# Forty-two split matmuls in the last block, and six sums moved within one early period

## The chip, the cores and the metric

The kernel runs on one core of one Trainium2 chip. The metric is the device time of one execution in microseconds, the median of several executions. A profile was taken of one execution of each kernel. Its times are counted from the first instruction, and its span leaves out about 2 us of the execution that lie outside the program's own instructions.

## The reference

A dense layer, an exact GELU, and a second dense layer:

```python
def reference(x, w1, b1, w2):           # x 16 x 512 x 768, w1 768 x 3072, w2 3072 x 768, fp32
    y = np.matmul(x, w1) + b1
    y = 0.5 * y * (1.0 + erf(y / np.sqrt(2.0)))
    return np.matmul(y, w2).astype(np.float32)
```

## The kernel before

The kernel works in fp16 and saves matmuls by a Strassen scheme: seven products in place of eight, with sums of blocks made on VectorE (DVE). The rows go in eight blocks of 1024 (`sb`). In a block (the first two differ in part) stage 1 has twelve units (`k`) of seven products, each three matmuls of 512 columns. The last stage has seven units of seven products, each twelve matmuls of 192 columns. TensorE (PE) runs the products in periods that mix the unit `i` that begins with the unit `j` that ends:

```python
def period(i, j, fill):            # (cut: special cases)
    p1(i); copy_xy(i)              # bank bX, then bX copied into bY
    p7(j); fill(1)                 # bank bY of j, then add_c22 reads it
    p5(i); fill(2)                 # bW
    p3(j); fill(3)                 # bZ, then a sum reads it
    p6(i); j.right_done(); fill(4) # bank bY of i; then it is copied into bZ
    p4(j); fill(5)                 # bY of j
    p2(i); fill(6)                 # bX
```

`fill(slot)` puts work for DVE and the queues between the products. DVE takes its work in the order of the program, as the DVE lines of e1 below show, where a copy stands behind sums that waited 1.19 us for a load. These sums belong to one early period, the one before W1 tile 6 is first used (`at[1, 0]` is 7, so the period is `pos == 5`):

```python
if slot == (1 if pos < at[1, 0] else 4) and pos + 1 < len(seq) and seq[pos + 1][0] == 0:
    prep_wt(seq[pos + 1][1])                       # 4 sums of the next W1 tile
...
if slot == 1:
    if pos == at[1, 0] - 2:
        x_sums(1, soon, slice(0, RH // 2), (0, 1)) # 2 sums of x of block 1
```

The last unit of the last block (`ends`) writes its results out in pieces as they are done:

```python
def p3(u):                                         # (cut)
    u.mm(3, bZ, False, 0, u.C)
    nc.vector.tensor_tensor(out=u.c12(), ...)
    if u.ends:
        u.store(0)                                 # 384 KB, nc.sync
...
def last(self, banks):                             # (cut) the last two stores, 96 KB each
    (nc.sync, nc.scalar)[t].dma_start(out=orr[...], in_=o)
```

Of the kernel before, what the change touches and what calls it, by code (L numbers as in the profile page):

```python
# [22 lines left out]
def kernel(  # L23
# [8 lines left out]
    nc = tc.nc  # L32
# [5 lines left out]
    RH = SB // 2  # L38
    nsb = R // SB
# [81 lines left out]
    def w1_op(wt, slot):  # L121
        raw = wt[:, 0:4 * KQ * P].rearrange("p (a k b c) -> p a b k c", a=2, k=KQ, b=2)
        if slot in RAW:
            return raw[:, RAW[slot][0], RAW[slot][1]]
        return wt[:, slot * KQ * P:(slot + 1) * KQ * P].rearrange("p (k c) -> p k c", c=P)
# [79 lines left out]
    with tc.manual_schedule():  # L205

        soon, queue, late, slow = [], [], [], []

        def tt(o, a, b, op):
            nc.vector.tensor_tensor(out=o, in0=a, in1=b, op=op)  # L210

        def later(n, f, q=None):
            (queue if q is None else q).append((70 + n * 0.52, f))

        def sums(ns):

            for q in (soon, queue):
                while q and ns >= q[0][0] * 0.6:
                    ns -= q[0][0]
                    q.pop(0)[1]()  # L220

        def flush(q):
            while q:
                q.pop(0)[1]()
# [18 lines left out]
        def keep(n):  # L243
            nc.sync.dma_start(out=w1s[hi_of(n)][:], in_=wts[n])

        def prep_wt(n, ks=()):
            o = {s: w1_op(wts[n], s) for s in range(7)}
            early = ((T3, B22, T1, SUB), (T2, T3, B11, ADD), (T4, B21, T2, SUB), (T1, T1, B11, SUB))
            usual = ((T3, B22, T1, SUB), (T1, T1, B11, SUB), (T2, B22, T1, SUB), (T4, B21, T2, SUB))
            for d, a, b, op in [early[k] for k in ks] if ks else usual:  # L250
                later(KQ * P, lambda d=d, a=a, b=b, op=op: tt(o[d], o[a], o[b], op), soon)
# [6 lines left out]
        def prep_w2(d, c, q):  # L258
            a, b = {T1: (T3, B11), T2: (B22, T1), T3: (B22, T3), T4: (B21, T2)}[d]
            o = [w2v[s][:, :, c:c + W2C, :] for s in (d, a, b)]  # L260
            later(2 * W2C * N4, lambda: tt(*o, SUB), q)
# [69 lines left out]
        def transpose_pe(sb, t, copy=nc.scalar.copy):  # L331
            for kc in range(2 * KQ):
                nc.tensor.transpose(out=bT[t % 2][:, kc, :], in_=xhs[t][:, kc * P:(kc + 1) * P],
                                    identity=ident[:])
            copy(out=xT_of(sb, t), in_=bT[t % 2][:])  # L335

        def blocks(sb):
            XT = XTs[sb]
            return [XT[:, a, c:c + KQ, :] for a in range(2) for c in (0, KQ)]

        def x_sums(sb, q, r=slice(0, RH), ks=range(4)):
            A11, A12, A21, A22 = [a[:, :, r] for a in blocks(sb)]
            S1, S2, S4 = [a[:, :, r] for a in XSs[sb]]
            n = KQ * len(range(RH)[r])
            ops = ((S1, A21, A22, ADD), (S2, S1, A11, SUB), (A21, A11, A21, SUB), (S4, A12, S2, SUB))
            for k in ks:
                later(n, lambda k=k: tt(*ops[k]), q)

        def g_sum(k, U, c0=0, c1=NH, q=None):
            G1, G2 = g_of(U // NU)  # L350
            r = slice(U % NU * P, (U % NU + 1) * P)
            g11, g21 = G1[:, c0:c1, 0, r], G1[:, c0:c1, 1, r]
            g12, g22 = G2[:, c0:c1, 0, r], G2[:, c0:c1, 1, r]
            s = [t[:, c0:c1, :] for t in GS]
            a, b, op = ((g21, g22, ADD), (s[0], g11, SUB), (g11, g21, SUB), (g12, s[1], SUB))[k]
            later((c1 - c0) * P, lambda: tt(s[k], a, b, op), q)
# [40 lines left out]
        class Unit1:  # L397
# [11 lines left out]
            def mm(self, p, dst, first, c0, c1):  # L409
                A11, A12, A21, A22 = blocks(self.sb)  # L410
                a, slot = {1: (A11, B11), 2: (A12, B21), 3: (self.XS[2], B22), 4: (A22, T4),
                           5: (self.XS[0], T1), 6: (self.XS[1], T2), 7: (A21, T3)}[p]
                for c in range(c0, c1):
                    nc.tensor.matmul(out=dst[:, 0:RH], lhsT=w1_op(self.wt, slot)[:, c, :],  # L414
                                     rhs=a[:, c, :], start=first and c == 0,
                                     stop=c == self.C - 1, skip_group_check=True)

            def alloc(self):
                self.tmp = (tmps1 if self.sb < ONE else
# [325 lines left out]
        for half in range(2):  # L745
            r = slice(half * KQ, (half + 1) * KQ)
# [36 lines left out]
        def plain(n, row, side, half, r=slice(0, RH)):  # L783
            slot = ((B11, T1), (B21, B22))[half][side]
            for c in range(KQ):
                nc.tensor.matmul(out=banks[n, row][side][:, r], lhsT=w1_op(wts[n], slot)[:, c, :],
                                 rhs=blocks(0)[2 * row + half][:, c, r],
                                 start=half == 0 and c == 0 and r.start == 0,
                                 stop=half == 1 and c == KQ - 1, skip_group_check=True)

        def plain_done(n, row, side):
            nc.scalar.activation(out=Gs[0][side][:, n, row, :], in_=banks[n, row][side][:, 0:RH],
                                 func=GELU, bias=b1t[:, 2 * n + side:2 * n + side + 1])
# [41 lines left out]
        for k in (2, 3):  # L835
            for r in (top, bottom):
# [5 lines left out]
        seq = ([(0, k) for k in range(7)] +  # L842
               [(1, 0), (1, 1), (1, 2), (0, 7), (1, 3), (0, 8), (1, 4), (0, 9), (1, 6), (0, 10), (0, 11),
                (1, 5), (1, 10), (1, 11), (1, 7), (1, 8), (1, 9)])
        at = {u: n for n, u in enumerate(seq)}
# [10 lines left out]
        def loads_a(pos):  # L856
            if pos == 0:
                load_wt(4)
                load_next_x(1, (0, 4, 1, 5))
                load_wt(5)  # L860
                load_next_x(1, (2, 6, 3, 7))
                load_wt(6)
            for n in range(7, NH):
                if pos == at[1, over[n]] + 1:
                    load_wt(n)
            if pos in w2_at_pos:
                load_w2(*w2_at_pos[pos])
# [6 lines left out]
        def transposes_a(pos):  # L874
            for t in (pos - 1, pos + 3):
                if t not in X1_PE:
                    transpose_dma(1, t)

        def fill_a(pos, slot):
            if pos == 2 and slot == 1:  # L880
                plain(1, 1, 1, 1, bottom)
                plain_done(1, 1, 1)
            if (pos, slot) in X1_AT:
                transpose_pe(1, X1_PE[X1_AT.index((pos, slot))])
            if pos == at[1, 0] - 1 and slot == 2:
                x_sums(1, soon, slice(RH // 2, RH), (0, 1))
            if slot == (1 if pos < at[1, 0] else 4) and pos + 1 < len(seq) and seq[pos + 1][0] == 0:
                prep_wt(seq[pos + 1][1])
            if slot == 4:
                if pos in (3, 4):  # L890
                    prep_wt(pos - 3, (3,))
                for m, c in ((21, 9), (22, 0), (23, 3), (23, 6)):
                    if pos == m:
                        prep_w2(T2, c, queue)
                        prep_w2(T3, c, late if m == 23 else queue)
                if pos == 23:
                    for c in range(0, NH, W2C):
                        prep_w2(T4, c, late)
            if slot == 1:
                if pos == at[1, 0] - 2:  # L900
                    x_sums(1, soon, slice(0, RH // 2), (0, 1))
                if pos == at[1, 0]:
                    x_sums(1, soon, ks=(2, 3))
                if pos == at[0, NH - 1] + 2:
                    for c in range(0, NH, W2C):
                        prep_w2(T1, c, queue)
                    for k in (0, 1):
                        g_sum(k, 0)
            if pos > at[0, NH - 1]:
                if slot in (1, 4):  # L910
                    sums((0, 1100, 0, 0, 1500)[slot])
            elif slot in (1, 2, 4, 5):
                sums((0, 600, 300, 0, 600, 300)[slot])
            if slot == 5:
                loads_a(pos)
                if pos < 5:
                    transposes_a(pos)
                for n in KEEP.get(pos, ()):
                    keep(n)
            if slot == 6:  # L920
                flush(soon)
# [256 lines left out]
```

## Time and profile before

| | kernel before |
|---|---|
| time, median of 6 runs (3 of them known at the prediction) | 852.37 us (852.18 to 852.68) |
| span of the profiled execution | 850.53 us |
| TensorE busy | 842.8 us, 99% |
| start of the last matmul | 845.02 us |
| last part of the last store landed | 849.44 us |
| last instruction fetch of TensorE | 844.30 us, 16,384 bytes, 1.24 us |

In the trace the landing of each of the last eight stores is told by 16 updates of its semaphore (a counter that other work waits for). I read them as 16 parts, one for each DMA engine; the prediction names the page that says so. The time between the fifteenth and the sixteenth update is then the time for which one engine alone holds up the whole transfer; I call it the gap.

### The profile page before, as it was taken

What the parts mean: (1) busy time and instruction counts of PE and PEld (TensorE: products, weight loads), DVE (VectorE), ACT (ScalarE), POOL (GpSimd) and SP (SyncE); (2) the same over time, 40 slices, a digit from 0 to 9 for tenths busy, and PEclk for the clock granted to TensorE, in tenths of its full rate; (3) what the DMA queues carried; (4) which work ended last, traced back from release to release, by engine and by line L of the source; (5) the groups of instructions that cost most, each with busy time, mean ns of one, the idle gap of its engine ahead of it and who ended that gap; (6) DMA issues with size and microseconds to landing.
All of it is one profiled execution on the core that took longest, in us unless ns stands there. A gap on an engine that the chain in (4) does not pass through costs nothing.

```text
span 850.5 us, 16682 instructions
## 1 busy us (share of the span) xinstructions
PE 842.8 (99%) x6504; PEld 573.4 (67%) x6504; DVE 673.3 (79%) x1134; ACT 426.3 (50%) x700; POOL 94.8 (11%) x151
## 2 busy tenths in 40 slices
PE   8999999999999999999999999999999999999997
PEld 5444445796544897449964599545995469944797
DVE  5766679777857997679967799668996699957997
ACT  4777763231287413773247721577126861277511
POOL 5021100042200002000020000210002100010000
PEclk9999999999999999999999999999999999999999
DMA  9998796699998699977999599995999949984497
GB/s 224 203 282 173 163 222 230 235 203 219 368 340 185 216 338 364 290 163 266 335 366 292 125 298 342 360 288 108 316 350 347 259 143 323 359 308 146 122 316 255
DMA packets 144819, 222.11 MB, mean 261 GB/s; under 512 B 61964, under 2 KB 85444, under 8 KB 144740
## 3 DMA queue, kind: packets, MB, share of 16 engines
q1 hardware_dynamic: 117392, 178.85, 66.6%
q0 software_dynamic: 27168, 42.08, 22.3%
q8 instruction: 51, 0.84, 0.4%
q14 instruction: 28, 0.23, 0.1%
q10 hardware_dynamic: 180, 0.11, 0.0%
HBM read 181.78 MB, written 49.45 MB: 272 GB/s over the span
## 4 chain that ended last, share of the span: by engine, by line
PE 98%; DMA 1%; ACT 0%; DVE 0%; SPq 0%; issue 0%
PE bY L414 21%; PE bY L518 15%; PE bX L414 14%; PE bX L518 10%; PE bW L414 7%; PE bZ L414 7%; PE bZ L518 5%; PE bW L518 5%; PE bY L457 4%; PE bZ L457 2%; PE bW L457 2%; PE bY L606 2%; PE bX L606 1%; PE bX L457 1%; DMA arena<-in_x_dram 1%; PE bZ L606 1%
## 5 line engine op out<-in xcount | busy, mean ns | idle before, releaser
L210 DVE TENSOR_TENSOR arena<-arena 128x1536 f16<-128x1536 f16 (+6 forms) x638 | 410.1, 674 | 5.7 <-ACT arena L335 0.9
L414 PEld LDWEIGHTS <-arena 128*128 128x128 f16 x1974 | 192.5, 98 | 224.0 <-issue 0.2
L518 PEld LDWEIGHTS <-arena 128*128 128x128 f16 x3528 | 292.1, 98 | 8.2
L414 PE MATMUL bY<-arena 128*128 128x512 f16 x846 | 214.4, 379 | 0.0
L637 DVE TENSOR_TENSOR arena<-bY,arena 128x512 f32<-128x512 f32 (+1 forms) x102 | 69.4, 681 | 118.1 <-PE bY L414 88.0
L630 ACT COPY bY<-bX 128x512 f32<-128x512 f32 (+1 forms) x145 | 79.6, 549 | 118.1 <-DVE arena L567 87.9
L518 PE MATMUL bY<-arena 128*128 128x192 f16 x1500 | 138.3, 246 | 0.0
L414 PE MATMUL bX<-arena 128*128 128x512 f16 x564 | 138.2, 379 | 0.0
L430 ACT ACTIVATE arena<-arena,b1t 128x1024 f16<-128x1024 f32 x94 | 108.0, 1149 | 51.6 <-DVE arena L665 51.6
L650 ACT COPY arena<-bW 128x512 f32<-128x512 f32 (+1 forms) x149 | 81.9, 550 | 92.9 <-PE bW L518 43.9
L518 PE MATMUL bX<-arena 128*128 128x192 f16 x1020 | 93.1, 246 | 0.0
L665 DVE TENSOR_TENSOR arena<-bZ,arena 128x512 f32<-128x512 f32 (+1 forms) x102 | 69.3, 679 | 21.4 <-PE bZ L414 18.2
L550 POOL DMA_DIRECT2D out_dram<-arena x42 | 30.5, 728 | 409.7 <-DVE arena L661 374.1
L414 PE MATMUL bW<-arena 128*128 128x512 f16 x282 | 76.2, 379 | 0.0
L414 PE MATMUL bZ<-arena 128*128 128x512 f16 x282 | 76.2, 379 | 0.0
L681 ACT COPY bZ<-bY 128x512 f32<-128x512 f32 (+1 forms) x60 | 31.8, 529 | 80.8 <-PE bY L457 30.0
L435 ACT ACTIVATE arena<-bX,b1t 128x512 f16<-128x512 f32 x94 | 64.0, 680 | 9.8 <-PE bX L414 9.7
L435 ACT ACTIVATE arena<-bY,b1t 128x512 f16<-128x512 f32 x94 | 63.3, 674 | 0.0
L457 PEld LDWEIGHTS <-arena 128*128 128x128 f16 x432 | 42.2, 98 | 28.0 <-issue 0.2
L319 POOL DMA_DIRECT2D arena<-in_x_dram x60 | 33.5, 626 | 156.3 <-DMA arena<-arena 146.9
L518 PE MATMUL bZ<-arena 128*128 128x192 f16 x504 | 48.5, 246 | 0.0
L518 PE MATMUL bW<-arena 128*128 128x192 f16 x504 | 48.5, 246 | 0.0
(63 smaller groups left out, 426.4 us busy)
## 6 DMA issues: line engine op xcount, KB each, us to landing
arena<-w2s SPq DMA_DIRECT2D x299, 288.0 KB, 4.6
arena<-w1s SPq DMA_DIRECT2D x72, 672.0 KB, 6.8
out_dram<-arena POOLq DMA_DIRECT2D x46, 384.0 KB, 7.1
w2s<-arena SPq DMA_DIRECT2D x49, 288.0 KB, 4.4
arena<-in_x_dram POOLq DMA_DIRECT2D x60, 192.0 KB, 7.7
w1s<-arena SPq DMA_DIRECT2D x12, 672.0 KB, 6.6
arena<-in_w_dram POOLq DMA_DIRECT2D x17, 384.0 KB, 8.4
out_dram<-arena SPq DMA_DIRECT2D x13, 384.0 KB, 2.5
```

Source lines behind the costliest of these rows:

```text
L210: nc.vector.tensor_tensor(out=o, in0=a, in1=b, op=op)
L319: nc.gpsimd.dma_start(out=xhs[t], in_=xr[:, sb * 8 + t, :])
L414: nc.tensor.matmul(out=dst[:, 0:RH], lhsT=w1_op(self.wt, slot)[:, c, :], rhs=a[:, c, :], start=first and c == 0, stop=c == self.C - 1, ski ...
L430: nc.scalar.activation(out=self.G[1][:, hi, :, :], in_=self.tmp, func=GELU, bias=b1t[:, 2 * hi + 1:2 * hi + 2])
L435: nc.scalar.activation(out=self.G[0][:, hi, row, :], in_=bank[:, 0:RH], func=GELU, bias=b1t[:, 2 * hi:2 * hi + 1])
L457: nc.tensor.matmul(out=dst[:, 0:N2], lhsT=a, rhs=w[:, :, c, :], start=first and c == 0, stop=c == self.C - 1, skip_group_check=True)
L518: nc.tensor.matmul(out=dst[:, t * N4:(t + 1) * N4], lhsT=a, rhs=w[:, c, :], start=first and c == 0 and t == ts[0], stop=c == NQ - 1, skip_ ...
L606: nc.tensor.matmul(out=dst[:, t * N4:(t + 1) * N4], lhsT=a, rhs=self.w[q][:, c, :], start=first and c == 0 and t == 0, stop=c == NQ - 1, s ...
L630: nc.scalar.copy(out=bY[u.g % 2][:, 0:u.F], in_=bX[u.g % 2][:, 0:u.F])
L637: nc.vector.tensor_tensor(out=u.c22(), in0=bY[u.g % 2][:, 0:u.F], in1=w[:, 0:u.F], op=ADD)
L650: nc.scalar.copy(out=w[:, 0:u.F], in_=bW[:, 0:u.F])
L665: nc.vector.tensor_tensor(out=u.c12(), in0=bZ[:, 0:u.F], in1=w[:, 0:u.F], op=ADD)
```

## The change

Its intent, in its own words, is "to shift instruction fetches". Two units of the last block run each matmul of 512 columns as two of 256, which adds 84 instructions to TensorE's stream. Besides, the sums of W1 tile 6 and of x(1) come later in their period.

```diff
+                w = RH // (2 if self.sb + 1 == nsb and self.k in (1, 2) else 1)
                 for c in range(c0, c1):
-                    nc.tensor.matmul(out=dst[:, 0:RH], lhsT=w1_op(self.wt, slot)[:, c, :],
-                                     rhs=a[:, c, :], start=first and c == 0,
-                                     stop=c == self.C - 1, skip_group_check=True)
+                    for r in range(0, RH, w):
+                        nc.tensor.matmul(out=dst[:, r:r + w], lhsT=w1_op(self.wt, slot)[:, c, :],
+                                         rhs=a[:, c, r:r + w], start=first and c == 0 and r == 0,
+                                         stop=c == self.C - 1, skip_group_check=True)
...
-            if slot == (1 if pos < at[1, 0] else 4) and pos + 1 < len(seq) and seq[pos + 1][0] == 0:
+            if slot == (1 if pos < at[1, 0] and pos != at[1, 0] - 2 else 4) and pos + 1 < len(seq) and seq[pos + 1][0] == 0:
                 prep_wt(seq[pos + 1][1])
...
+            if pos == at[1, 0] - 2 and slot == 4:
+                x_sums(1, soon, slice(0, RH // 2), (0, 1))
             if slot == 1:
-                if pos == at[1, 0] - 2:
-                    x_sums(1, soon, slice(0, RH // 2), (0, 1))
```

## The prediction

> **What bounds the kernel now.** I read the page's busy table first, then its chain of work that ended last, then the waits of TensorE, then the stretches of the last 12 us. Busy share and chain agree:
>
> ```profile
> span 850.5 us, 16682 instructions
> PE 842.8 (99%) x6504; PEld 573.4 (67%) x6504; DVE 673.3 (79%) x1134; ACT 426.3 (50%) x700; POOL 94.8 (11%) x151
> PE 98%; DMA 1%; ACT 0%; DVE 0%; SPq 0%; issue 0%
> ```
>
> A busy TensorE is not proof of a full one, because matmuls overlap. So I looked at its waits (waiter, what it waited for, us in total, times, longest) and at the spacing of its instructions in the timeline:
>
> ```profile
> PE bX L764 <- DVE arena L750: 1.2, 1, 1.2
> PE bT L333 <- DVE arena L770: 0.7, 1, 0.7
> PE bT L333 <- ACT arena L335: 0.4, 1, 0.4
> ```
>
> These three are all of its waits, and all lie in the first 10 us. From the first product to the last, six matmuls of 512 columns start 1.29 us apart (215.7 ns each) and 24 of 192 columns 1.98 us (82.5 ns each). Summed over the whole trace, the starts after 10 us are less than 1 us late against those two rates. So nothing in the middle can be gained by moving waits about. What is left is the head, which the change doesn't touch, and the tail after the last matmul (845.02 us): some 5.5 us of a last sum, the last stores and the ending.
>
> The tail, as busy time in chosen stretches (columns: stretch, length, busy of PE, weight loads, DVE, ACT, POOL, granted clock, DMA share, GB/s):
>
> ```profile
> 838.60:840.50 1.90, 1.90 (x26) 1.90 (x25) 1.90 (x4) 0.25 (x1) 0.00 (x0) 1.00 0.00 0
> 840.70:841.70 1.00, 1.00 (x15) 1.00 (x13) 0.90 (x3) 0.00 (x0) 0.00 (x0) 1.00 0.95 347
> 842.00:844.20 2.20, 2.20 (x30) 2.20 (x27) 1.85 (x5) 0.00 (x0) 0.00 (x0) 1.00 1.03 365
> ...
> 845.90:846.40 0.50, 0.00 (x0) 0.00 (x0) 0.00 (x0) 0.00 (x0) 0.00 (x0) 1.00 0.05 15
> 846.60:848.10 1.50, 0.00 (x0) 0.00 (x0) 0.00 (x0) 0.00 (x0) 0.00 (x0) 0.87 1.02 350
> 848.30:848.90 0.60, 0.00 (x0) 0.00 (x0) 0.00 (x0) 0.00 (x0) 0.00 (x0) 0.50 0.07 23
> ```
>
> A share of 0.05 to 0.07 is one DMA engine of 16. So at 845.9 and again at 848.3 fifteen engines are done and a single one works on, and the kernel ends with that one. The landings say the same. Of the store issued at 842.54, 15 parts land by 845.60 and the sixteenth at 847.39 (1.79 us later); of the next (843.91) the gap is 1.68; of the last three it is 0.73, 0.76 and 0.79, the very last part landing at 849.44 instead of 848.65. The cause I read in the DMA packets: in 842 to 852 us there is one packet of the instruction queue, 16,384 bytes, at 844.30, taking 1.24 us. The page counts them:
>
> ```profile
> q8 instruction: 51, 0.84, 0.4%
> ```
>
> The trace doesn't name the engine of a packet, so that the late engine is the one with the fetch is inferred. But the earlier fetches show the same thing: after those at 812.03 and 833.41 the last part of the next transfers lands 1.49 and 1.02 us after the fifteenth, against some 0.1 us in transfers far from a fetch.
>
> **What the Trainium skill says.** (1) "Runtime: NRT & Kernel Launch", Instruction fetch mechanics: instructions stream in through a DMA queue of the sequencer's own, in blocks of 16 KiB, which are 256 instructions, and a crossing is mostly hidden. The trace agrees on the size: 51 packets of 16,384 bytes, some 256 TensorE instructions apart, for 13,022 built ones (50.9 blocks). It is hidden from TensorE, but the tail shows it not hidden from a store. (2) "DMA: Bandwidth & Descriptors", Queues, rings and completion order: each DMA engine takes its queue rows in turn, whole packets at a time. That fits one engine held up by one fetch. (3) Same page, Why a DMA increments its semaphore by 16 and not by 1: only the full count means landed, so one late engine makes the whole store late; the 1.79 us gap is that. (4) "TensorE: Matmul & The Clock Gate", Wait — 56ns, not 53.3ns?: a matmul's spacing is its columns at 2.4 GHz plus about 2.5 ns. The trace agrees: 215.7 ns for 512, 82.5 for 192.
>
> **The change, part by part.** *Split matmuls.* Two units (k = 1, 2) of the last block have 7 products of 3 matmuls, 42 in all. Each becomes two of 256 columns: 42 matmuls and, in the built program, 42 weight loads more, 84 instructions. The cost: the 48 matmuls of 256 columns that the kernel already has (the start's) are spaced 109.2 ns, with weight loads of 98 ns in between that keep up. Two of them take 218.4 against 215.7, so 2.6 ns for each split matmul, times 42: **+0.11 us**, all of it on the path.
>
> *What the 84 instructions move.* Fetches come at fixed counts in the stream: the last four stood at 12,220, 12,474, 12,736 and 13,001 TensorE instructions started, so the last one should again come near 13,001. That was 20 instructions before the end; now it is 104. 84 instructions are 42 matmuls of 192 columns, 42 x 82.5 ns = 3.46 us earlier against the tail: at 840.8 on the old clock. There is no 52nd fetch: one block more would come near 13,257, and the stream ends at 13,106.
>
> At 840.8 the fetch meets the first of the last stores (DMA share 0.95) and delays one engine by what the others cost: 1.0 to 1.8 us. Before the last stores that engine can catch up wherever the other 15 idle. The old tail shows how much: from the store of 843.91 to that of 844.90 the gap shrank from 1.68 to 0.73, so 0.95 us, at the lull between 845.83 and 846.46. The new place adds the lull at 841.75 to 841.95, 0.2 us. Together 1.15 us. What remains at the end is 0 (fetch costs 1.0) to 0.65 us (it costs 1.8); I take 0.25, as the nearest fetches (1.02 and 1.49) are nearer the low end. In place of 0.79 us that makes **-0.54 us**, an estimate from the landings.
>
> *Sums moved within one early period.* In the built order, DVE's four sums of W1 tile 6 and the two of x(1) stand behind the two PSUM operations of their period instead of in front of and between them; no other engine's order changes (but for the longer PE stream). Before:
>
> ```profile
> 36.38 1.14 DVE L210 TENSOR_TENSOR arena<-arena 128x384 f16<-128x384 f16 x3 [0.66 <-DMA arena<-in_w_dram]
> 37.44 0.68 DVE L665 TENSOR_TENSOR arena<-bZ,arena 128x512 f32<-128x512 f32 x1
> 38.23 0.70 DVE L683 COPY bZ<-bY 128x512 f32<-128x512 f32 x1
> 38.84 1.41 DVE L210 TENSOR_TENSOR arena<-arena 128x384 f16<-128x384 f16 x3
> ```
>
> DVE waits 0.66 us for the tile's load there, with the copy into bZ queued behind. But that copy ends at 38.93 and TensorE writes bZ again at 40.61, so 1.7 us of slack, and no wait of TensorE is on the list. After: the sum from bZ runs near 36.6, the copy near 37.3, then four sums of 0.38 us and two of 0.56, ending near 40.6. T1 of tile 6 is ready near 38.8 and first used by TensorE at 39.97; the sum on bY that follows (old start 40.16) starts some 0.4 us later and ends near 41.3, and TensorE touches that bank again at 41.9. All fits. The worth in these runs: **0.0 us**. What it buys is tolerance of a late load, which the three runs (852.32 to 852.53) don't show to be needed.
>
> Sum: 852.42 + 0.11 - 0.54 + 0.0 = 851.99, say 852.0 us.
>
> **The rivals.** *A: the fetch only changes its victim.* Between 841.95 and 845.83 all 16 engines are busy without a break, so a delay taken at 840.8 can't shrink there; if it costs 1.8 us, as the one at 844.30 did, 0.65 us remains and the change gains 0.14 - 0.11, nothing: 852.4. For it: the DMA share of 1.03. Against it: 0.2 us more to catch up in, and a fetch that mostly costs nearer 1 us.
>
> *B: the late engine leaves altogether.* With a fetch that costs 1.1 us or less the whole 0.79 goes: 852.42 + 0.11 - 0.79 = 851.74. This is the floor, as the last store's other 15 parts land at 848.65 whatever the fetch does.
>
> *C: TensorE loses more than 0.11 us.* The split units double the weight loads in their 9 us, and DVE's later sums come within 0.7 us of the bank that TensorE wants. Weight loads of 98 ns against 109 of matmul speak against the first; that it would be one wait of some tenths, against a large second. It would give 852.6 to 853.0.
>
> *D: the fetches of the last block, all moved, delay a weight load.* Those loads are issued some ten products ahead (10 x 0.99 us) and land in 4.6 us, so 1.5 us of delay is hidden.
>
> **Range and chances.** B's floor with the run-to-run 0.1 us sets 851.55 at the low end; A with part of C sets 852.65 at the high end. Nearly all of what I can imagine lies within 1 us, and 2% would be 17 us, so the chances are 0.01 faster, 0.98 within 2%, 0.01 slower.
>
> **What would show it.** In the new profile: 6546 matmuls; TensorE's last matmul about 0.11 us later; one instruction packet near 840.9 and none after; the last store's sixteenth part within 0.4 us of the fifteenth, and a DMA share near 0 in the stretch after most parts landed; DVE's wait for the W1 load gone, and TensorE's waits still only those of the first 10 us. The prediction is wrong if the last fetch falls elsewhere than 3.5 us earlier, if a late engine remains although the fetch has moved (then the fetch wasn't its cause), or if TensorE shows a new wait near 40 us or in the last block.

## The result, and the profile after

| | before | after |
|---|---|---|
| time, median | 852.37 us (6 runs, 852.18 to 852.68) | 851.36 us (6 runs, 850.89 to 851.60) |
| span of the profiled execution | 850.53 | 848.74 |
| start of the last matmul | 845.02 | 844.64 |
| last store landed | 849.44 | 847.59 |
| from the last matmul's start to the last landing | 4.42 | 2.95 |
| last fetch, against the start of the last matmul | 0.73 earlier | 5.44 earlier |
| gap of the last three stores | 0.73, 0.76, 0.79 | 0.02, 0.04, 0.03 |

The ratio is 0.9987, with a 95% interval of 0.9974 to 1.0: the same within 2%. (Ratios are the mean time of one kernel's fast runs over that of the other's of the same rounds, so not quite the ratio of the medians.) The gain is 1.01 us by the medians. I had said 0.4 us, in a range from 851.55 to 852.65 us; what failed in the working is said further below.

The busy table of the page has hardly moved:

```profile
span 848.7 us, 16767 instructions
...
PE 843.3 (99%) x6546; PEld 577.6 (68%) x6546; DVE 673.5 (79%) x1134; ACT 426.4 (50%) x700; POOL 94.9 (11%) x151
```

The stretches of the tail have. These answer to the six that the prediction shows (stretch, length, busy time of PE, weight loads, DVE, ACT and POOL, granted clock, DMA share, GB/s):

```profile
838.20:840.10 1.90, 1.90 (x26) 1.90 (x24) 1.90 (x4) 0.27 (x1) 0.00 (x0) 1.00 0.04 9
840.30:841.30 1.00, 1.00 (x15) 1.00 (x13) 0.90 (x3) 0.00 (x0) 0.00 (x0) 1.00 0.95 344
841.60:843.80 2.20, 2.20 (x29) 2.20 (x28) 1.84 (x5) 0.00 (x0) 0.00 (x0) 1.00 1.01 363
...
845.50:846.00 0.50, 0.00 (x0) 0.00 (x0) 0.00 (x0) 0.00 (x0) 0.00 (x0) 1.00 1.02 359
846.00:847.10 1.10, 0.00 (x0) 0.00 (x0) 0.00 (x0) 0.00 (x0) 0.00 (x0) 1.00 0.98 340
847.30:847.90 0.60, 0.00 (x0) 0.00 (x0) 0.00 (x0) 0.00 (x0) 0.00 (x0) 1.00 0.00 0
```

Three things are to be seen. In the quiet stretch before the last stores one engine is now at work, where before there was none; the view of DMA queues for that stretch says what it does:

```profile
DMA packets 1, 0.02 MB, mean 9 GB/s; under 512 B 0, under 2 KB 0, under 8 KB 0
...
q8 instruction: 1, 0.02, 3.8%
```

It is the last fetch, alone (839.20, taking 1.15 us). Secondly, the end with one engine at work is gone: 0.00 in place of 0.07. Thirdly, so is the lull of the 15 other engines (0.05 before, at 845.90 to 846.40); at the same point of the tail the share is now 1.02. The timeline of SyncE's issues tells why the lull went. The first lines are the kernel before's (start, us, what):

```profile
844.90 1.04 SPq L550 DMA_DIRECT2D out_dram<-arena  x1
846.04 0.42 SPq L529 DMA_DIRECT2D out_dram<-arena  x1
```

And the changed kernel's:

```profile
844.52 0.37 SPq L552 DMA_DIRECT2D out_dram<-arena  x1
844.98 0.44 SPq L531 DMA_DIRECT2D out_dram<-arena  x1
```

The same store of 384 KB took 1.04 us to issue before and takes 0.37 now, and the one behind it is issued some 0.7 us sooner after the last matmul.

The spans differ by 1.79 us, more than the medians do. By matching the same matmul in both traces: 0.54 us of the difference arose before the sixty-first matmul, up to where the two programs are the same. In all 14 profiles the sixty-first matmul starts anywhere from 12.89 to 13.97 us, as the first loads land sooner or later; the profiled execution of the changed kernel was an early one and its fastest (850.89). At 43 to 45 us it lost 0.11 us in two late starts, the first 0.05 us after the end of the next copy out of bank bY, and in the two split units 0.09 us. The last matmul then came 0.39 us sooner, and the tail behind it was 1.47 us shorter.

### The profile page after: what moved, and what is told of

It reads as the page before. It is cut to its first block, busy times and chain, and to the rows that moved or that the text cites. A ratio compares the mean times of both kernels' runs of the same rounds, so it can differ in the third digit from the quotient of the medians.

```text
span 848.7 us, 16767 instructions
## 1 busy us (share of the span) xinstructions
PE 843.3 (99%) x6546; PEld 577.6 (68%) x6546; DVE 673.5 (79%) x1134; ACT 426.4 (50%) x700; POOL 94.9 (11%) x151
## 4 chain that ended last, share of the span: by engine, by line
PE 99%; DMA 1%; SPq 0%; DVE 0%; ACT 0%; issue 0%
PE bY L416 22%; PE bY L520 15%; PE bX L416 14%; PE bX L520 10%; PE bZ L416 7%; PE bW L416 7%; PE bZ L520 5%; PE bW L520 5%; PE bY L459 4%; PE bZ L459 2%; PE bW L459 2%; PE bY L608 2%; PE bX L608 1%; PE bX L459 1%; DMA arena<-in_x_dram 1%; PE bZ L608 1%
## 5 line engine op out<-in xcount | busy, mean ns | idle before, releaser
L416 PE MATMUL bY<-arena 128*128 128x512 f16 (+1 forms) x864 | 214.5, 375 | 0.0
L416 PE MATMUL bX<-arena 128*128 128x512 f16 (+1 forms) x576 | 138.3, 375 | 0.0
L416 PE MATMUL bZ<-arena 128*128 128x512 f16 (+1 forms) x288 | 76.2, 375 | 0.0
L416 PE MATMUL bW<-arena 128*128 128x512 f16 (+1 forms) x288 | 76.2, 375 | 0.0
```

What stands on the lines that cost most here:

```text
L416: nc.tensor.matmul(out=dst[:, r:r + w], lhsT=w1_op(self.wt, slot)[:, c, :], rhs=a[:, c, r:r + w], start=first and c == 0 and r == 0, stop= ...
```

## The experiments

The theory (F): the last instruction fetch of TensorE stood among the last stores and held up one DMA engine, and through it everything behind; the 84 instructions moved it into a quiet stretch. The rivals: the gain comes from the moved sums (S), or from the matmuls of 256 columns themselves (M). All kernels were correct. "Tail" is the time from the last matmul's start to the last landing in the profiled execution.

| run | median us | before in the same rounds | ratio (95%) | last fetch before last matmul | gap of the last store | tail |
|---|---|---|---|---|---|---|
| e1 split only | 851.62 | 852.34 | 0.9987 (0.9974 to 1.0001) | 5.26 us | 0.01 | 2.94 |
| e2 sums only | 852.25 | 852.34 | 1.0000 (0.9987 to 1.0012) | 0.61 | 0.69 | 4.09 |
| e3 six units split | 852.60 | 852.34 | 1.0001 (0.9988 to 1.0013) | 0.46 | 1.25 | 4.20 |
| e4 84 empty instructions | 851.49 | 852.34 | 0.9990 (0.9978 to 1.0003) | 5.41 | 0.02 | 2.95 |
| e5 42 empty instructions | 851.87 | 852.26 | 0.9995 (0.9982 to 1.0008) | 3.03 | 0.60 | 3.66 |
| e6 84 empty, sums moved | 851.04 | 852.26 | 0.9985 (0.9972 to 0.9997) | 5.35 | 0.01 | 2.94 |
| e7 late tile, old order | 855.73 | 852.26 | 1.0052 (1.0038 to 1.0066) | 0.77 | 0.70 | 3.92 |
| e8 late tile, new order | 854.85 | 852.26 | 1.0033 (1.0021 to 1.0046) | 0.35 | 1.46 | 4.33 |
| e9 less late, old order | 853.59 | 852.62 | 1.0011 (0.9999 to 1.0022) | 0.37 | 1.34 | 4.31 |
| e10 less late, new order | 853.03 | 852.62 | 1.0007 (0.9994 to 1.0021) | 0.74 | 0.80 | 4.42 |
| e11 a store from ScalarE's queue | 852.47 | 852.62 | 0.9996 (0.9984 to 1.0008) | 0.66 | 1.13 | 4.14 |
| e12 84 empty in block 2, sums moved | 851.24 | 852.62 | 0.9979 (0.9967 to 0.9991) | 4.87 | 0.11 | 3.11 |

The intervals are as wide as the gain, so the times alone decide little (only e6 and e12 among the faster ones have an interval clear of 1). The traces do: where the last fetch stands 0.35 to 0.77 us before the last matmul (eight kernels, with the one before) the tail is 3.92 to 4.42 us; where it stands 4.87 to 5.44 us before (five kernels) the tail is 2.94 to 3.11.

That the late engine is the one with the fetch stays inferred, as the trace names no engine. The landings fit it: in each of the eight profiles with a late fetch, the two stores that landed before the fetch began have gaps of at most 0.04 us, and the large gaps open with the stores under way during it. In the eight, in e5 and in e12 one issue of the tail took 0.53 to 1.13 us; in the other four, whose largest gap in the tail was 0.25 to 0.56 us, none took over 0.45.

**e1: the split alone.**

```diff
+                w = RH // (2 if self.sb + 1 == nsb and self.k in (1, 2) else 1)
 (the matmuls as in the change; the sums stay where they were)
```

> The change's 84 instructions alone, sums left in their old place. Theory F (the last instruction fetch is moved out of the last stores): the whole gain stays, 851.1 to 851.4 us against 852.4 of the kernel before, the last store's sixteenth part lands within 0.1 us of the fifteenth, and the last but one store is issued in about 0.4 us instead of 1.04. Theory S (the gain comes from the sums moved in the first block): no gain, 852.4 to 852.6.

The gap and the issue time came as F says (0.01 us; the store issued in 0.37 us). The time, 851.62, missed the expected 851.1 to 851.4. Its profile shows a wait of TensorE that neither the kernel before nor the changed one had (waits of TensorE; then its timeline and DVE's):

```profile
PE bY L416 <- DVE bZ L685: 0.4, 1, 0.4
```

```profile
37.68 1.46 PE L416 MATMUL bX<-arena 128*128 128x512 f16 x6
39.50 0.81 PE L416 MATMUL bY<-arena 128*128 128x512 f16 x3 [0.37 <-DVE bZ L685]
```

```profile
36.91 1.14 DVE L210 TENSOR_TENSOR arena<-arena 128x384 f16<-128x384 f16 x3 [1.19 <-DMA arena<-in_w_dram]
37.97 0.68 DVE L667 TENSOR_TENSOR arena<-bZ,arena 128x512 f32<-128x512 f32 x1
38.75 0.70 DVE L685 COPY bZ<-bY 128x512 f32<-128x512 f32 x1
```

DVE waited 1.19 us for W1 tile 6 here (0.66 in the kernel before), the copy out of bY ended at 39.45, and the next matmul into bY started at 39.50, 0.53 us later than in step. This is what moving the sums can save, and e7 to e10 test it.

**e2: the sums alone.**

```diff
-                w = RH // (2 if self.sb + 1 == nsb and self.k in (1, 2) else 1)
+                w = RH // (2 if False else 1)          # in the changed kernel
```

> The sums moved alone, no matmul split. Theory F: 852.3 to 852.6 us, as before; the last fetch again near 844 us, the last store's sixteenth part again 0.6 to 0.9 us after the fifteenth; perhaps 0.1 us lost near 44 us, where the changed kernel's TensorE started two matmuls 0.03 and 0.08 us late. Theory S: 851.2 to 851.6.

852.25 us, fetch at 844.29, gap 0.69: as F says, so S is not the source of the gain. The 0.1 us at 44 us didn't appear, so it isn't a fixed cost of the order.

**e3: six units split.**

```diff
+                w = RH // (2 if self.sb + 1 == nsb and self.k in range(1, 7) else 1)
```

> Six units of the last block split instead of two: 252 instructions more, four short of one fetch block of 256, so the last fetch (one more, the 52nd) falls again about 20 instructions before the end. Theory F: the gain is gone though three times as many matmuls are split: 852.5 to 852.8 us (0.27 us of it the splitting), a late sixteenth part of 0.6 us or more again. Theory M (matmuls of 256 columns help by themselves, say by freeing banks or the clock): 851.4 or less.

The last fetch came when 13,259 of TensorE's instructions had started (13,001 in the kernel before, 258 earlier) and 0.46 us before the last matmul, the gap is 1.25 us, the time 852.60. Three times the splitting and no gain: M falls, and a shift of 252 instructions brings the fetch back to within 0.3 us of its old place, as a period of 256 would. The splitting of 126 matmuls cost 0.29 us between the first and the last matmul of the block, 2.3 ns each. The end of the tail, with one engine at work for longer than before:

```profile
848.10:848.90 0.80, 0.00 (x0) 0.00 (x0) 0.00 (x0) 0.00 (x0) 0.00 (x0) 1.00 0.07 23
```

In this run the store before the last two was issued in 0.37 us; the wait moved into the gap (1.34, 1.28, 1.25 where the kernel before had 0.73, 0.76, 0.79), and the tail was as long. With its sums in the old order, e3 also lost 0.19 us at the place where e1 lost 0.53: the copy out of bY ended at 38.79 us and the next matmul into bY started at 38.84.

**e4: empty instructions.**

```diff
+                if self.sb + 1 == nsb:                 # once per product, 84 in all
+                    for _ in range(1):
+                        nc.tensor.nop(hint='shift', nofuse=True)
```

> The old matmuls, and 84 empty instructions put into TensorE's stream over the last block's first stage (one for each product), sums in the old place: the same shift of the stream without a matmul split. Theory F: the gain of the changed kernel or some 0.1 us more, 851.0 to 851.3 us, last fetch near 839 to 841 us, sixteenth part within 0.1 us. Theory M: no gain, 852.4. If an empty instruction costs TensorE time, the last matmul starts later than 845.0 on the scale of the start of the last block.

Fetch, gap and tail are the changed kernel's (5.41 us, 0.02, 2.95) with no matmul split, and TensorE started nothing late for the empty instructions: from the first to the last matmul of the block it kept the step of the kernel before within 0.01 us. The median, 851.49, is 0.2 above the range that I expected; the profiled execution took 850.98.

**e5: half the shift.**

```diff
+                if self.sb + 1 == nsb and self.k < 6:  # 42 in all
+                    for _ in range(1):
+                        nc.tensor.nop(hint='shift', nofuse=True)
```

> 42 empty instructions instead of 84: the last fetch moves half as far, to 841.3 to 842.6 us on the scale of the kernel before, where the last stores keep all DMA engines busy. Theory F with the late engine never catching up: no gain or nearly none, 852.1 to 852.5 us; from the last matmul's start to the last landing 3.9 to 4.5 us, as in the kernel before (4.42), against 2.95 in the kernels whose last fetch fell into the quiet stretch. Theory L (the gain grows with the shift, each us of shift letting the engine catch up more): half the gain, 851.8 to 852.0, and 3.5 to 3.8 us.

851.87 us, a tail of 3.66 and a gap of 0.60: L's numbers. The late engine does catch up: its gap was 1.31 us in the first store after the fetch, then 1.20, 0.86, 0.75, 0.65, 0.62 and 0.60. The largest step, 1.20 to 0.86, is at a store whose issue took 1.13 us, so there again part of the catching up is the other engines being held: the fifteen parts of that store landed 0.19 us later after the last matmul than in the changed kernel (0.78 us against 0.59). The rest, some 0.5 us, I put down to what the stores leave free; in 842 to 844 us the DMA share was 0.91. So rival A's "can't shrink there" and my version of F were both too strict.

**e6: empty instructions and moved sums.** The edit is that of e4 together with the change's sums.

> Candidate for the best: 84 empty instructions in place of the split matmuls, and the sums moved as in the change. No TensorE cost of splitting (0.1 us) and no wait near 39 us: 850.9 to 851.3 us, at or just below the changed kernel's 851.36. TensorE waits only in the first 14 us; 2.9 to 3.0 us from the last matmul to the last landing.

851.04 us (850.68 to 851.21), with a ratio whose interval is clear of 1. It has the lowest median of all and no wait of TensorE after the start. That it beats the changed kernel (851.36, on other rounds) by the 0.1 us of the splitting is not resolved by these runs.

**e7 and e8: a late tile.** One load of 384 KB more, into a place not yet used, ahead of that of W1 tile 6; e7 has the old order of the sums, e8 the new one.

```diff
+                nc.gpsimd.dma_start(out=w1_raw(wt_at(o_w2)), in_=w1r[:, :, 12 * P:14 * P])
                 load_wt(6)
```

> The kernel before with one more load of 384 KB (into a place not used yet, result unchanged) ahead of the load of W1 tile 6, so that the tile lands 0.8 to 2 us later. Theory B (the sums in the old place hold back the copy out of bank bY, which TensorE needs some 0.05 us after it is done): TensorE waits near 39 us for the copy by as much as the tile is late, 0.8 to 2 us, and the time rises by that to 853.0 to 854.3. Theory N, as predicted before the result (1.7 us of slack): at most 0.3 us more, 852.3 to 852.7.

> The same late load, with the sums moved as in the change and no matmul split. Theory B: the copies no longer stand behind the tile, so TensorE waits 0 to 0.5 us near 39 us and the time is 852.2 to 852.8, at least 0.6 us under the one with the old order. Theory N: both orders alike within 0.3 us.

The delay was larger than meant, and both times missed what I expected: the tile landed at 39.2 us in both, not at 36.4. Now both had to wait for the tile itself, and for the copy. The waits of TensorE, e7 first:

```profile
PE bY L414 <- DVE bZ L683: 1.8, 1, 1.8
...
PE bX L414 <- DMA arena<-in_w_dram: 0.3, 1, 0.3
```

```profile
PE bX L416 <- DMA arena<-in_w_dram: 1.3, 1, 1.3
...
PE bY L416 <- DVE bZ L685: 0.9, 1, 0.9
```

The old order is 0.88 us slower by the medians, but as a test of the old order alone this is inconclusive, since another limit took over.

**e9 and e10: a tile less late.** As e7 and e8 with two of six row blocks of the extra load.

```diff
+                nc.gpsimd.dma_start(out=w1_raw(wt_at(o_w2))[:, 0:2], in_=w1r[:, 0:2, 12 * P:14 * P])
                 load_wt(6)
```

> As the late load before, a third as large (two of six row blocks, 128 KB), sums in the old place: the tile should land some 1 us later, near 37.1 us. Theory B (bank bY): TensorE waits 0.5 to 1.2 us near 39 us for the copy, and the time is 852.7 to 853.6. Theory N (1.7 us of slack): no wait, 852.1 to 852.5.

> The same smaller late load with the sums moved: by theory B the copy is done near 37.5 us and the tile is needed only near 39 us, so TensorE waits nowhere after 14 us: 852.0 to 852.5, at least 0.4 us under the old order. Theory N: the same as the old order.

The tile landed at 37.36 and 37.03. The same two products in e9 and in e10 (timeline of TensorE):

```profile
38.14 1.46 PE L414 MATMUL bX<-arena 128*128 128x512 f16 x6
39.99 0.81 PE L414 MATMUL bY<-arena 128*128 128x512 f16 x3 [0.38 <-DVE bZ L683]
```

```profile
37.77 1.46 PE L416 MATMUL bX<-arena 128*128 128x512 f16 x6
39.07 0.81 PE L416 MATMUL bY<-arena 128*128 128x512 f16 x3
```

With the old order the matmul into bY starts 1.85 us after the group before it, with the new one 1.30, as in step: 0.55 us saved at that point. (The medians differ by 0.56, but the intervals overlap.) That settles which bank matters. e9's time is at the upper end of what I expected, e10's 0.5 us above it. For e10 the trace shows where: three starts late by 0.54 us in all between 44 and 58 us. The first of them, late by 0.22 us, begins 0.05 us after the end of the next copy out of bY (44.10 us), and one of 0.08 us follows 2 us later; e9 has no late start there. So the new order gave back part of what it had saved. (e9's profiled execution, at 855.14 the slowest of its five, also waited 1.5 us for a weight tile at 483.7 us, which says nothing on the sums.)

**e11: one store from another queue.**

```diff
                 eng = nc.sync if self.sb + 1 == nsb and self.p != 2 else nc.gpsimd
+                if self.ends:
+                    eng = nc.scalar
```

> The kernel before with one of its last stores (384 KB, issued at 844.90 in 1.04 us) issued from ScalarE's queue. Theory H (the late engine's backlog holds up the issue on SyncE's queue, and the lull of the other 15 engines at 845.9 is that hold, not spare time in which the late one catches up): that store is issued in about 0.4 us, its 15 parts land some 0.5 us sooner after the last matmul, the sixteenth where it did, so its gap grows from 0.73 to 1.2 to 1.5 us, and the time stays 852.0 to 852.5. Theory C (the hold is a second cost beside the late engine): the last landing comes 0.5 us sooner, 851.7 to 851.9.

The store was issued in 0.43 us, its first 15 parts landed 2.42 us after the last matmul's start (3.28 in the kernel before), its gap grew from 0.73 to 1.23, and the tail was 4.14 us, within what kernels with a late fetch show; the time 852.47. In the place of the lull the DMA share was 0.67 and not 0.05:

```profile
846.00:846.30 0.30, 0.00 (x0) 0.00 (x0) 0.03 (x1) 0.00 (x0) 0.00 (x0) 1.00 0.67 190
...
848.20:849.00 0.80, 0.00 (x0) 0.00 (x0) 0.00 (x0) 0.00 (x0) 0.00 (x0) 1.00 0.07 24
```

So H fits and C doesn't: with the hold gone before this store the fifteen engines are free earlier, and the sixteenth still ends the kernel. The tail is 0.28 us shorter than that of the kernel before, but 0.19 us of it stood already in the largest gap ahead of this store (1.60 against 1.79). The hold didn't go altogether: the next store on SyncE's queue took 0.67 us to issue. That the hold comes about as the late engine's backlog fills what SyncE's queue may have under way is inferred. The Trainium skill, "Perfetto Trace Analysis", DMA Instruction — HWDGE (DVE, Sync), has the profiled time of an issue run until all its descriptors are made, and a buffer of them that can be full. The 1.04 and 0.37 us fit that; no run shows the buffer.

**e12: the shift elsewhere.** The edit of e6 with `self.sb == 2`.

> 84 empty instructions in block 2 instead of the last one, sums moved. Theory F asks only for the count of instructions ahead of the last fetch, not for where they stand: last fetch again 5.2 to 5.6 us before the last matmul, 2.9 to 3.0 us to the last landing, 850.8 to 851.3 us. If what matters is something in the last block: 852.0 to 852.4.

851.24 us, though the 84 instructions now stand some 570 to 630 us before the end (at 221 to 283 us). The last fetch came 4.87 us before the last matmul, a little later than I expected, and kept a gap of 0.11 us and a tail of 3.11. It is the count of instructions that matters, not their place. This run also shows that the new order isn't free of the danger: TensorE waited 0.3 us near 44 us for the next such copy out of bY (ended 43.93, matmul at 43.98), and two starts there were 0.51 us late in all.

## Why the prediction was wrong, point by point

- **What bounds the kernel: right.** In the middle the changed kernel lost 0.20 us; the gain is in the tail, by the last fetch. e1, e3, e4 and e12 show it from four sides.
- **Split matmuls, +0.11 us: right.** Measured 0.09 us in the changed kernel (42 matmuls), 0.08 in e1.
- **The last fetch at 840.8: wrong.** The step that failed was "the last one should again come near 13,001", so that 84 instructions would move it by 3.46 us. It came when 12,970 had started, 5.44 us before the last matmul, a shift of 4.71 us: the 31 instructions fewer are another 1.28 us at 82.5 ns for a matmul and its weight load. So the count isn't fixed. It was 12,970 to 12,974 in the changed kernel, e1, e4 and e6, 12,982 and 12,986 in e12 and e5, and 12,999 to 13,009 in the seven others with 51 fetches. A reading that fits is that the fetch follows TensorE's sequencer, which is ahead of the started instructions by an amount that varies along the stream; no run shows the sequencer, so the cause stays open. The fetch then met not the first of the last stores but the quiet stretch ahead of them, and cost only that first store a gap of 0.42 us.
- **The remaining gap of 0.25 us: wrong with it.** Measured 0.02 to 0.04 us.
- **"In place of 0.79 us": the mis-sized term.** I took the gap of the last store for all that the fetch cost. The tail shows 1.47 us in the changed kernel; a fetch at the end costs 1.0 to 1.5 (3.92 to 4.42 against 2.94 or 2.95). I read the lull at 845.83 to 846.46 as time in which the late engine caught up with fifteen idle ones. They were idle because the issue of their next store took 1.04 us in place of 0.37, so the lull was part of the cost. The landings say so too: the fifteenth part of that store landed 3.28 us after the last matmul's start before the change and 2.34 after it, so nearly all of the 0.95 us by which the gap shrank is fifteen parts that came later. Of the 1.47 us by which the very last landing moved, 0.71 are the fifteen parts of the last store, which landed later, and only 0.76 are its gap. e11 took the hold away from that store and e3 happened to have none before it: the last gap was 1.13 and 1.25 us and the tail stayed at 4.14 and 4.20. The floor of rival B, "whatever the fetch does", fell for the same reason: with nothing left of the gap the prediction's own sum ends at 851.74, above the measured 851.36. In the prediction's own sum this term was 0.68 us too small, and the remaining gap 0.22 us too large; both make the predicted gain too small.
- **Rival A: not tested by the change itself,** as the fetch fell elsewhere. e5 is its case, and half of the gain was there.
- **Rivals C and D: small or not seen.** Besides the 0.09 us of splitting, C got 0.11 us, from the two late starts at 43 to 45 us. Of D there is nothing: after 46 us no start of TensorE in either kernel is over 0.09 us late.
- **Sums, 0.0 us: wrong in the reason.** I looked for the next writer of bank bZ (40.61) and found 1.7 us of slack. The copy out of bY is also waited for by the next product into bY, at 38.98, and it ended at 38.93. In e1 and e9, where TensorE did wait for it, the matmul followed 0.05 us after the copy's end; so the kernel before had nothing to spare. The changed kernel's copy ends at 37.54 and the product comes at 38.44. The product in the kernel before, then copy and product in the changed one (the copy before is in the prediction's lines):

```profile
38.98 0.81 PE L414 MATMUL bY<-arena 128*128 128x512 f16 x3
```

```profile
36.84 0.70 DVE L685 COPY bZ<-bY 128x512 f32<-128x512 f32 x1
...
38.44 0.81 PE L416 MATMUL bY<-arena 128*128 128x512 f16 x3
```

What the move is worth varies with the landings. Of the six kernels with the old order and no extra load, e1 lost 0.53 us and e3 0.19 near 39 us, the kernel before, e4, e5 and e11 nothing. Of the four with the new order, the changed kernel lost 0.11 us and e12 0.51 near 44 us, e2 and e6 nothing. So the move takes the danger from one copy and can leave it with the next, and a gain on average isn't shown. e2's median is 0.09 us under that of the kernel before, which these rounds don't resolve.

The sum of these measured parts, by the tail and the splitting alone, is 0.09 - 1.47 = -1.38 us; the medians give -1.01. A tail with a late fetch is 4.23 us in the mean of its eight profiles (4.42 was at their upper end), so -1.2 is the better number for it. The remaining 0.2 us is less than what one kernel's executions differ by.

## What to carry to other kernels

When a kernel ends with stores, look in the DMA packets for an instruction fetch among them, and compare the landing of the fifteenth and the sixteenth part of each transfer: one late part points to one late engine. A few empty instructions anywhere in the stream move the fetch, at no cost that these runs could show, but the count has to be found by trying, and a later edit of the stream undoes it. And before taking an engine's idle time as spare time, ask whether the late one caused it; before calling a copy slack, look at the next writer of what it reads as well as of what it writes.

## What the Trainium skill lacked or had wrong

- "Runtime: NRT & Kernel Launch", Instruction fetch mechanics: it calls the cost of a block boundary mostly hidden. The runs agree for TensorE, but a fetch among the last stores lengthened the tail from 2.95 to as much as 4.42 us.
- The same section has the next block fetched while the current one is executed, but doesn't say at which point of it. In the runs the last fetch came at 12,970 to 13,009 started instructions where there were 51 of them, and at 13,259 with 252 instructions more, so counting didn't place it to within 1 us here.
- "DMA: Bandwidth & Descriptors", Queues, rings and completion order: it describes the turns of queues on one engine, but not what one 16 KiB fetch costs a store behind it. In the nine profiles whose last fetch fell among the stores in full flow, the largest gap of a store was 1.31 to 1.82 us; in the five whose fetch began in or next to the quiet stretch it was 0.25 to 0.82.
- No page that I read says that one late engine lengthens the issue of the next store: 1.04 us against 0.37. That the engine causes it is inferred, from the ten profiles named above.
